# Strassen for half of a right-half stage in a 2048 x 2048 matmul with RMS norm, with B's sums and the loads of A moved to make room

## The chip, the cores and the metric

One core of one Trainium2 chip. The metric is the device time of the kernel in microseconds (us). The kernel before takes 224.39 us, the median of 3 runs (224.3 to 224.49). The engines are named as in the profile: PE is TensorE (matmuls), DVE is VectorE, ACT is ScalarE, POOL is GpSimd and SP is SyncE, which here only issues DMAs: the DMA transposes, nearly all stores of the result, and one load at the start.

## The reference

```python
# a: 2048 x 2048, b: 2048 x 2048, gamma: 2048, all float32; eps = 1e-5
def reference(a, b, gamma, eps):
    x = np.matmul(a, b)
    rms = np.sqrt(np.mean(x ** 2, axis=-1, keepdims=True) + eps)
    return (gamma * x / rms).astype(np.float32)
```

## The kernel before

A has 16 row blocks of 128 rows. The result has four chunks of 512 columns; chunks 0 and 1 are the left half, 2 and 3 the right half. A matmul takes a 128x128 block of A (transposed) and 128x512 of B.

The kernel has three parts. In the **left stage** row blocks 0 to 3 are multiplied with the left half of B as it arrives from memory. In the **right stage** the same row blocks are multiplied with the right half of B, again as it arrives. After that all of B is resident, and the row blocks 4/5, 6/7, ... 14/15 are computed in **pairs** by Strassen's scheme: a pair of row blocks and one half of the columns form a 2x2 matrix of 1024-deep pieces, and seven products of 8 matmuls replace eight. "Pair 4/5, second half" below means row blocks 4 and 5 with the right half of B.

The products are the usual ones: product 1 is (A11+A22)(B11+B22), 2 is (A21+A22)B11, 3 is A11(B12-B22), 4 is A22(B21-B11), 5 is (A11+A12)B22, 6 is (A21-A11)(B11+B12), 7 is (A12-A22)(B21+B22). So each pair needs sums of A (`a_sums`, VectorE), and each half of B needs sums of B once. Sums for products 1, 3 and 4 are kept apart (`b_sums`); those for 6 and 7 overwrite B12 and B21 in place (`b_sums_in_place`) when nothing needs the original any more.

The right stage of before, which the change replaces:

```python
    later = ([("b", kp) for kp in range(5)]
             + [("a", HB), ("b", 5), ("b", 6), ("a", HB + 1), ("b", 7)])   # order of loads
    ...
    groups2 = [(r, c) for r in range(HB) for c in (2, 3)][:-1]
    for kp in range(KP):                     # KP = 8 pieces of B's right half
        load_later(1)
        ...
        stream(groups2, kp, before)          # 14 plain matmuls per piece
        square(squares[kp][0], x_chunk(*squares[kp]))
        ...                                  # sums of B
    ...
    bank = new_bank()                        # the last group, 16 matmuls, after the others
    for kt in range(KT):
        ...
        head_matmul(bank, r3, 3, kt)
    ...
    finish(0, (1, 0))                        # scale and store row block 0
```

One Strassen pair. A bank is a PSUM accumulator of 128x512; `hooks` puts the work for other row blocks between the products, and so fixes its place in the order of each engine:

```python
    def group_half(g, j, hooks):
        x11, x12, x21, x22 = (...)           # the four 128x512 chunks of the result
        t = x22
        at_hook(0)
        p2, p5 = new_bank(), new_bank()
        product(g, j, 2, p2)
        c = spare if (g, j) == (G0, 0) else t
        nc.scalar.copy(out=c, in_=p2)                                      # ScalarE
        ...
        product(g, j, 5, p5)
        nc.vector.tensor_tensor(out=t, in0=p5, in1=c, op=ALU.add)          # VectorE
        ...
        p1 = new_bank()
        product(g, j, 1, p1)
        nc.vector.tensor_tensor(out=t, in0=p1, in1=t, op=ALU.subtract)
        at_hook(3)
        product(g, j, 4, p2, start=False)    # accumulates onto p2, after the copy above
        nc.scalar.copy(out=x21, in_=p2)
        ...
        product(g, j, 3, p5, start=False)    # accumulates onto p5, after the add above
        ...
```

The two reuses of a bank: product 4 may start only when ScalarE has copied product 2, and product 3 only when VectorE has added product 5.

The preparation of a later row block, and its place in pair 4/5:

```python
    def row_norm(mb):     # ScalarE: sum of squares of the block's rows, square root
    def row_factor(mb):   # VectorE: a power of two for each row
    def row_apply(mb):    # ScalarE: scale the rows to fp16
    def apply(mb):
        row_apply(mb)
        transpose_dma(mb)                    # nc.sync.dma_start_transpose
    ...
                hook(0, row_factor, nxt)     # nxt = 6, in the first half of pair 4/5
                hook(1, row_norm, nxt + 1)
                hook(1, apply, nxt)
                hook(2, a_sums, g, (7, 6))
                hook(2, row_factor, nxt + 1)
                hook(2, finish, 1)
                hook(3, squares2, 2)
                hook(4, apply, nxt + 1)      # block 7's DMA transpose
                hook(4, finish, 2)
    ...
    def load_after(g, mb):                   # in the second half: A of blocks 8 and 9
        wait_for(x_chunk(2 * g + 1, 1)[:, 0:1])
        load_block(mb)
```

`finish(mb)` takes the root of the row's mean square (`take_rms`: a reduction on VectorE, a root on ScalarE), scales both halves by it and by gamma (two VectorE instructions of 1.28 us) and stores them through SP.

## Time and profile before

| | before |
|---|---|
| time, median | 224.39 us |
| span of the profiled run | 222.6 us |
| PE busy | 211.1 us, 95% of the span |
| pair 4/5 starts on PE | 69.25 us |
| pair 6/7 starts on PE | 93.63 us |

From the page of the kernel before: busy time by engine, the clock granted to TensorE in 40 slices of the span (9 is full), and the chain of work that ended last, by engine and by line.

```profile
PE 211.1 (95%) x1043; PEld 98.6 (44%) x1043; DVE 161.8 (73%) x324; ACT 129.1 (58%) x272; POOL 24.5 (11%) x49
PEclk9999999999999999999999999999999999999997
PE 83%; DMA 8%; DVE 2%; POOL 2%; issue 1%; ACT 1%; DVEq 0%; ACTq 0%; POOLq 0%
```

The waits of PE in the kernel before: the line that waited, what for, then the total in us, how often, and the longest.

```profile
PE acc L138 <- DVE sq L129: 1.5, 1, 1.5
PE tbank L148 <- POOL msq L198: 1.2, 1, 1.2
PE acc L350 <- DMA b<-in_b_dram: 0.4, 1, 0.4
PE tbank L382 <- DVE head_at L170: 0.4, 1, 0.4
```

These are all at the start, the last ends at 24.7 us, and they sum to 3.5 us. After that the view lists no wait of PE, and its clock is full in every slice but the last. So the kernel is bound by PE: a matmul saved should show in the time, and so should any new wait.

The timeline of PE in the kernel before, around pair 4/5 (start and length in us, then the matmuls and their number):

```profile
69.25 3.62 PE L279 MATMUL acc<-b,s 128*128 128x512 bf16 x16
84.84 1.89 PE L279 MATMUL acc<-early,s 128*128 128x512 bf16 x8
86.57 3.77 PE L279 MATMUL acc<-early,at_even 128*128 128x512 bf16 x16
90.18 7.07 PE L279 MATMUL acc<-b,s 128*128 128x512 bf16 x32
97.08 1.89 PE L279 MATMUL acc<-t_left,s 128*128 128x512 bf16 x8
```

The first line is products 2 and 5 of pair 4/5, where the right stage has ended. The next three are its second half: product 1 at 84.84, products 4 and 3 at 86.57, and from 90.18 products 7 and 6, which are followed without a gap by products 2 and 5 of pair 6/7. Sixteen matmuls take 3.45 us, so pair 6/7 starts at 93.63. Product 1 of pair 6/7 starts at 97.08.

The two DMA transposes of row blocks 6 and 7 in the kernel before, as SP issued them (the second number is the time SP was held):

```profile
77.38 2.03 SPq L186 DMA_TRANSPOSE head_at<-head_at  x1
82.89 1.71 SPq L186 DMA_TRANSPOSE head_at<-head_at  x1
```

By the trace's records of landings, block 7's landed at 87.18, 4.3 us after its issue and 6.4 us before pair 6/7 starts. The loads of A that follow were issued after that, at 88.37. A later transpose of the same size met such loads (a line of SP's timeline and one of POOL's, the kernel before):

```profile
108.41 3.40 SPq L186 DMA_TRANSPOSE at_even<-head_at  x1
110.44 1.05 POOL L115 DMA_DIRECT2D a<-in_a_dram  x2 [0.37 <-issue]
```

This one landed at 116.38, 8.0 us after its issue. It cost PE nothing there, as its rows were not wanted yet.

### The profile page before, as it was taken

Reading aid. Unit: us, or ns where it says so; the run is one execution under the profiler, and the core shown is the slowest. Engines: PE = TensorE matmul, PEld = TensorE weight load, DVE = VectorE, ACT = ScalarE, POOL = GpSimd, SP = SyncE. Lnnn points to the kernel's source line nnn. Section 1 sums busy time; section 2 is a strip of 40 time slices with the busy share of each in tenths; the row PEclk is TensorE's granted clock in tenths of the full one; section 3 lists DMA queues with packets and bytes.
Section 4 is the critical chain, followed back from the end, with each engine's and each line's share of the span. In section 5 each row is a group of like instructions: output and inputs, shape, how many; then the busy total and the mean of one; then the engine's idle time right before and its main releaser. Section 6 shows DMA issues by size and latency. Waiting matters only on the chain.

```text
span 222.6 us, 3026 instructions
## 1 busy us (share of the span) xinstructions
PE 211.1 (95%) x1043; PEld 98.6 (44%) x1043; DVE 161.8 (73%) x324; ACT 129.1 (58%) x272; POOL 24.5 (11%) x49
## 2 busy tenths in 40 slices
PE   7899999999999999999999999999999999999950
PEld 2445444444454444444444444444444444444430
DVE  2427557983999989978949298837994589587692
ACT  3110002807698895799646985699478954334570
POOL 7534232300000001000100002000200000000000
PEclk9999999999999999999999999999999999999997
DMA  6999999999973499818889259945994794044045
GB/s 184 223 202 209 203 208 211 212 303 259 327 280 159 188 272 292 310 72 226 276 228 400 58 174 222 366 151 143 246 368 168 97 282 189 0 188 193 0 190 188
DMA packets 36176, 47.13 MB, mean 212 GB/s; under 512 B 21952, under 2 KB 26048, under 8 KB 34496
## 3 DMA queue, kind: packets, MB, share of 16 engines
q0 software_dynamic: 9648, 23.33, 41.6%
q1 hardware_dynamic: 26080, 22.29, 33.0%
q10 hardware_dynamic: 432, 1.31, 2.0%
q8 instruction: 8, 0.13, 0.2%
q14 instruction: 8, 0.07, 0.1%
HBM read 34.60 MB, written 16.78 MB: 231 GB/s over the span
## 4 chain that ended last, share of the span: by engine, by line
PE 83%; DMA 8%; DVE 2%; POOL 2%; issue 1%; ACT 1%; DVEq 0%; ACTq 0%; POOLq 0%
PE acc L279 63%; PE acc L350 18%; DMA b<-in_b_dram 8%; POOL early L106 1%; DVE x L617 1%; POOL b L100 1%; DVE x L620 1%; PE tbank L179 1%; PE tbank L382 1%; PE tbank L165 1%; ACT sq L291 0%; DVEq L732 0%; ACT sq L682 0%; DVE x L690 0%; DVE r L322 0%
## 5 line engine op out<-in xcount | busy, mean ns | idle before, releaser
L279 PE MATMUL acc<-b,s 128*128 128x512 bf16 x376 | 83.3, 379 | 0.0
L279 PEld LDWEIGHTS <-s 128*128 128x128 f16 x472 | 46.2, 98 | 55.7 <-DVE s L244 0.2
L350 PE MATMUL acc<-b,head_at 128*128 128x512 bf16 x240 | 55.1, 379 | 0.6 <-DMA b<-in_b_dram 0.4
L291 ACT ACTIVATE sq<-x 128x512 bf16<-128x512 f32 x62 | 39.1, 631 | 10.9 <-DVE x L520 5.1
L340 DVE SCALAR_TENSOR_TENSOR x<-x,r,gamma_sb 128x1024 f32<-128x1024 f32 x28 | 34.7, 1282 | 0.8
L209 ACT ACTIVATE sq<-a 128x1024 bf16<-128x1024 f32 x24 | 25.4, 1057 | 16.8 <-DMA a<-in_a_dram 16.4
L350 PEld LDWEIGHTS <-head_at 128*128 128x128 bf16 x240 | 22.9, 98 | 26.7 <-issue 1.1
L393 ACT COPY x<-acc 128x512 f32<-128x512 f32 x11 | 5.9, 591 | 25.1 <-PE acc L350 25.1
L231 ACT ACTIVATE head_at<-a,s 128x2048 f16<-128x2048 f32 x10 | 19.9, 1990 | 0.0
L279 PEld LDWEIGHTS <-at_even 128*128 128x128 f16 x96 | 9.4, 98 | 11.5 <-issue 0.4
L279 PEld LDWEIGHTS <-head_at 128*128 128x128 f16 x96 | 9.4, 98 | 11.3
L100 POOL DMA_DIRECT2D b<-in_b_dram x15 | 10.6, 708 | 16.0 <-DMA b<-in_b_dram 13.2
L217 DVE TENSOR_SCALAR s<-norm 128x1 f32<-128x1 f32 x12 | 1.8, 150 | 14.3 <-ACT norm L212 14.2
L244 DVE TENSOR_TENSOR s<-at_even 128x1024 f16<-128x1024 f16 x15 | 9.7, 684 | 2.8 <-DMA at_even<-head_at 2.8
L291 ACT ACTIVATION_READ_ACCUMULATOR sq<-x 128x1 f32 x62 | 11.7, 188 | 0.0
L279 PE MATMUL acc<-t_left,s 128*128 128x512 bf16 x48 | 11.3, 379 | 0.0
L279 PE MATMUL acc<-early,s 128*128 128x512 bf16 x48 | 11.3, 379 | 0.0
L279 PE MATMUL acc<-early,at_even 128*128 128x512 bf16 x48 | 11.0, 379 | 0.0
L279 PE MATMUL acc<-t_left,at_even 128*128 128x512 bf16 x48 | 10.9, 379 | 0.0
L509 ACT COPY x<-acc 128x512 f32<-128x512 f32 x10 | 5.7, 575 | 8.9 <-PE acc L279 8.9
L279 PE MATMUL acc<-t_left,head_at 128*128 128x512 bf16 x48 | 10.8, 379 | 0.0
L279 PE MATMUL acc<-early,head_at 128*128 128x512 bf16 x48 | 10.8, 379 | 0.0
(86 smaller groups left out, 205.8 us busy)
## 6 DMA issues: line engine op xcount, KB each, us to landing
out_dram<-x SPq DMA_DIRECT2D x30, 512.0 KB, 3.1
a<-in_a_dram POOLq DMA_DIRECT2D x12, 1024.0 KB, 8.5
b<-in_b_dram POOLq DMA_DIRECT2D x15, 512.0 KB, 17.1
early<-in_a_dram POOLq DMA_DIRECT2D x7, 256.0 KB, 14.8
early<-in_b_dram ACTq DMA_DIRECT2D x2, 512.0 KB, 5.9
gamma_sb<-in_gamma_dram POOLq DMA_DIRECT2D x1, 1024.0 KB, 19.9
out_dram<-x SPq DMA_DIRECT2D x3, 256.0 KB, 3.5
early<-in_a_dram SPq DMA_DIRECT2D x1, 512.0 KB, 5.7
```

Of the source, the lines that this page charges most:

```text
L100: nc.gpsimd.dma_start(out=raw[j][kp], in_=b[kp * W2:(kp + 1) * W2, j * HALF:(j + 1) * HALF].rearrange("(t p) n -> p t n", p=P))
L106: nc.gpsimd.dma_start(out=ah(kp), in_=a[0:HB * P, kp * W2:(kp + 1) * W2].rearrange("(r p) k -> p r k", p=P))
L165: nc.tensor.matmul(view[:, t, r, :], ah(kp)[:, r, t * P:(t + 1) * P], identity, is_transpose=True, start=(t == 0 and r == 0), stop=(t == 1 ...
L209: nc.scalar.activation(out=junk, in_=a32[mb][:, h * HALF:(h + 1) * HALF], func=ACTF.Square, scale=2.0 ** -8, accum_out=n2[:, h:h + 1])
L231: nc.scalar.activation(out=a16[mb], in_=a32.pop(mb), func=ACTF.Copy, scale=factor.pop(mb))
L244: nc.vector.tensor_tensor(out=s_sum[s], in0=x, in1=y, op=op)
L279: nc.tensor.matmul(bank, lhsT[:, kp, :], rhs, start=(start and kp == 0), stop=(kp == KP - 1), skip_group_check=not start)
L291: nc.scalar.activation(out=sq[:, 0:CH], in_=src, func=ACTF.Square, scale=inv_sqrt_n, accum_out=msq[mb][:, c:c + 1])
L340: nc.vector.scalar_tensor_tensor(out=x, in0=x, scalar=r, in1=gamma_sb[:, h * HALF:(h + 1) * HALF], op0=ALU.mult, op1=ALU.mult)
L350: nc.tensor.matmul(bank, head_at[:, kt, r, :], head_rhs(c, kt), start=(kt == 0), stop=(kt == KT - 1))
L393: copy(out=x_chunk(*g), in_=banks[g])
L509: nc.scalar.copy(out=x21, in_=p2)
```

## The change

The right stage computed 8 groups (4 row blocks, 2 chunks) with 16 matmuls each, 128 in all. The change computes row blocks 0 and 1 as before (64 matmuls) and row blocks 2 and 3 as a Strassen pair (7 x 8 = 56): 120 matmuls, 8 fewer. Of its seven products, 2, 5 and 1 need no finished in-place sums, so they stream with B as it lands; 4, 3, 7 and 6 come after the last piece. To have time for the sums on VectorE, the in-place sums of B's left half move into the left stage. B's right half is loaded before row blocks 4 and 5, not interleaved with them; so the preparation of 4 and 5, the squares, and everything queued behind them, moves later. The core of the diff:

```diff
-    later = ([("b", kp) for kp in range(5)]
-             + [("a", HB), ("b", 5), ("b", 6), ("a", HB + 1), ("b", 7)])
+    later = [("b", kp) for kp in range(KP)] + [("a", n) for n in range(4)]
 ...
         if kp > 0:
             b_sums(0, kp - 1)
+        if 0 < kp < KP - 2:
+            b_sums_in_place(0, kp - 1)
+        if kp == 4:
+            a_sums(PAIR, (2, 5, 1), 0, 5)
 ...
+    def stream_right(kp):
+        order = [(g, kt) for kt in (2 * kp, 2 * kp + 1) for g in plain]
+        ...
+            for m in (2, 5):
+                pair_matmul(m, kp)
+            if kp > 0:
+                pair_matmul(1, kp - 1)
 ...
+    product(PAIR, 1, 4, pair[2], start=False)
+    row_norm(HB)
+    row_norm(HB + 1)
+    ...
+    product(PAIR, 1, 3, pair[5], start=False)
+    row_apply(HB)
+    ...
+    product(PAIR, 1, 7, p7, within={5: [lambda: turn(HB, 0)]})
+    ...
+    product(PAIR, 1, 6, p6)
 ...
             if g == G0:
-                hook(0, row_factor, nxt)
-                hook(1, row_norm, nxt + 1)
-                hook(1, apply, nxt)
+                hook(0, pair_sums)
+                hook(1, square_half, 1, 1)
+                hook(1, row_norm, nxt)
+                hook(2, pair_ends)
                 hook(2, a_sums, g, (7, 6))
-                hook(2, row_factor, nxt + 1)
-                hook(2, finish, 1)
-                hook(3, squares2, 2)
-                hook(4, apply, nxt + 1)
-                hook(4, finish, 2)
-                hook(6, b_sum_7, 1, KP - 1)
+                hook(2, row_factor, nxt)
+                hook(2, row_norm, nxt + 1)
+                hook(2, apply, nxt)
+                hook(2, finish, 0, (1, 0))
+                hook(3, square_half, r2, 1)
+                hook(3, row_factor, nxt + 1)
+                hook(3, finish, 1)
+                hook(4, row_apply, nxt + 1)
+                hook(4, finish, r2)
+                hook(7, transpose_dma, nxt + 1)
```

The last line is a detail. In the first half of pair 4/5 the changed kernel keeps an intermediate (`t`, and the copy `c`) in `spare`, a buffer that lies inside `head_at`, in the space that block 7's transposed rows will fill. So block 7's DMA transpose can't be issued before the last VectorE add of that half has read it.

## The prediction

> **What bounds it now.** TensorE. The page gives PE 95% busy; the chain of waits follows PE without a gap from 24.7 to 209.5 us, 0.2158 us per 128x512 matmul (91 in 19.64 us). [...] PE's waits after 24.7 us are about zero, so every PE stall or saved matmul there counts in full. VectorE and ScalarE run at 85-95% between 60 and 110 us (table by windows).
>
> **What the change does.** The right half goes from 128 matmuls to 64 + 7x8 = 120: minus 8 x 0.216 = -1.7 us. Transposes (32) stay. B's right half now arrives before blocks 4, 5. One 1.28 us activation-table load leaves the middle; left in-place sums (0.68 us each) move into the first stage; b_sum_6 and b_sum_7 vanish.
>
> **Costs on the critical path** (estimates: durations from the trace of before, summed along each engine's order; [...] the trace shows no reordering there):
>
> 1. First stage: three 128x640 A sums (about 0.4 us each) stand on VectorE before the head-transpose copy. Its bank is needed 3.46 us into the 3.9 us iteration; the copy would end at 4.5. PE stall about 1.0 us.
> 2. Right stage: B lands every 2.48 us, PE uses 2.38; VectorE is full but keeps ahead. No stall. Block 4's scaling then ends about 0.7 us after PE wants to transpose it inside product 7: 0.5-0.8 us.
>    So block pair 4/5 starts about where it did (69.3 us): the gain is spent.
> 3. Pair 4/5 (start S). On ScalarE after product 5: copy, half square 1.18, both row norms 2.57 each, scaling 1.95; only then (S+10.8) the root for block 0. On VectorE finish(0) (2.5), a subtraction, row factor (0.7) and the sum for block 1 wait for it; ScalarE's next root waits for those, about 3 us idle (S+12 to S+15). Then finish(1), scaling of block 7, finish(2). The left half's evictions stand behind these, so in the second half product 4 waits for ScalarE's copy of product 2 (done S+20 to 21.7, wanted S+17.3), and product 3 for VectorE's add (done S+24.2, wanted S+19.0). Loss about 5.2 us.
> 4. Block 7's DMA transpose now starts only after the last add of the first half (S+24), together with the next A loads; it took 4.2-8.0 us in before. Next pair's A sums wait: 0-3 us, estimate 1.0.
>
> Sum: -1.7 + 1.0 + 0.7 + 5.2 + 1.0 = +6.2, giving about 230.4 us. Later groups repeat as before, shifted.
>
> **Predicted: 230.4 us, 80% range 226.5 to 233.5. Faster by over 2%: 0.02; within 2%: 0.22; slower by over 2%: 0.76.**
>
> **What would show it.** PE waits: about 1 us for the transposed head copy (first stage); under 1 us for block 4's scaled rows; several us on the copy of product 2 and the add of product 5 in pair 4/5's second half; perhaps 0-3 us before the next pair. ScalarE: a wait of about 3 us for the sum of squares of block 1. PE gap-free elsewhere, 8 matmuls fewer. PE busy share falls to about 92%.
>
> **What would make it wrong.** If blocks 6, 7 or the roots arrive earlier than my order says, or bank and buffer releases are looser, item 3 shrinks and the time is 224-226; without any stall it is 222.7. If block 7's transpose collides fully with loads, or blocks 6, 7 land after S+6, it is 232-234.

## The result, and the profile after

The changed kernel is correct and took 235.28 us, the median of 4 runs (234.22 to 235.55), beside 224.41 us for the kernel before on the same chip. The ratio is 1.0476, with a 95% interval of 1.0454 to 1.0499: slower by 4.8%. (A ratio here is the mean time of one kernel's fast runs over the mean of the other's of the same rounds, so it is not quite the ratio of the medians quoted.) The direction was predicted; the size was not: 235.28 lies above the range of 226.5 to 233.5.

From the page of the changed kernel:

```profile
PE 213.6 (91%) x1035; PEld 98.4 (42%) x1035; DVE 168.1 (72%) x331; ACT 128.0 (55%) x263; POOL 25.6 (11%) x55
PEclk9999999999999997988999999999999999999996
PE 50%; DMA 4%; DVE 3%; ACT 1%; issue 0%; DVEq 0%; ACTq 0%
```

PE has 8 instructions fewer, as intended, yet it was busy for 2.5 us longer. Here that points to the clock: the granted clock is below 9 in three slices of the middle. And the chain that ended last now runs through a DMA in the middle: the page's next line, by lines, puts its 4% down to `head_at<-head_at`, a transpose. (The 8% of before were the loads of B at the start.)

The waits of PE in the changed kernel that before had not (of the third line, 0.4 us stood in before too):

```profile
PE acc L288 <- ACT x L562: 3.9, 1, 3.9
PE acc L288 <- DVE s L263: 3.8, 1, 3.8
PE tbank L403 <- DVE head_at L176: 1.2, 2, 0.8
PE tbank L188 <- DVE head_at L243: 0.2, 1, 0.2
```

The timeline of PE in the changed kernel, at the marks shown of before (in square brackets: the idle time before the line, and what ended it):

```profile
68.89 3.73 PE L288 MATMUL acc<-b,s 128*128 128x512 bf16 x16
84.54 1.89 PE L288 MATMUL acc<-early,s 128*128 128x512 bf16 x8
90.36 5.31 PE L288 MATMUL acc<-early,at_even 128*128 128x512 bf16 x16 [3.93 <-ACT x L562]
95.50 3.62 PE L288 MATMUL acc<-b,s 128*128 128x512 bf16 x16
102.95 5.31 PE L288 MATMUL acc<-b,s 128*128 128x512 bf16 x16 [3.83 <-DVE s L263]
108.10 1.89 PE L288 MATMUL acc<-t_left,s 128*128 128x512 bf16 x8
```

Set beside the marks of before, these give the account of the loss:

| mark on PE | before | after | behind by | added in this step |
|---|---|---|---|---|
| pair 4/5 starts | 69.25 | 68.89 | -0.36 | -0.36 |
| pair 4/5, second half, product 7 starts | 90.18 | 95.50 | 5.32 | +5.68 |
| pair 6/7 starts | 93.63 | 102.95 | 9.32 | +4.00 |
| pair 6/7, product 1 starts | 97.08 | 108.10 | 11.02 | +1.70 |
| end of the span | 222.6 | 233.7 | 11.1 | +0.1 |

**The first stages (-0.36).** The 8 matmuls saved are worth 1.7 us, and most is spent at once: in the left stage PE waits 0.85 us at 33.0 us for the copy of a transposed block (`head_at L176`), behind the new sums of A on VectorE, and 0.24 us for block 4's scaled rows (`L243`).

**Pair 4/5 (+5.68).** In the second half product 4 could not start until ScalarE had copied product 2. The lines of ScalarE's waits (68 to 112 us) that lead there, in the changed kernel:

```profile
ACT rms L340 <- DVE tot L338: 3.1, 1, 3.1
ACT x L573 <- DMA out_dram<-x: 1.3, 1, 1.3
```

ScalarE waited from 80.7 to 83.8 us to take the root for block 1, since VectorE was scaling block 0 first, and then 1.3 us for a store to free a chunk. The copies of the left half, the scaling of block 7 and the copy that PE needs stand behind these in ScalarE's order, so the latter ran at 89.74. VectorE's add of product 5 (done 93.72) came later still, and product 3 started right after it, at 93.78.

**The start of pair 6/7 (+4.00).** VectorE waited 7.7 us for block 7's DMA transpose, and PE 3.83 us behind VectorE. VectorE's wait (68 to 112 us), SP's two issues of transposes, and the time from issue to landing of the one between 90 and 106 us (the last number), in the changed kernel:

```profile
DVE s L263 <- DMA head_at<-head_at: 7.7, 1, 7.7
79.61 2.09 SPq L198 DMA_TRANSPOSE head_at<-head_at  x1
93.19 2.05 SPq L198 DMA_TRANSPOSE head_at<-head_at  x1
head_at<-head_at SPq DMA_TRANSPOSE x1, 9.0
```

The transpose was issued at 93.19, after the last add, and landed at 102.17, 9.0 us later. The loads of A for blocks 8 and 9 were issued at 93.72, beside it, and landed at 101.53 and 104.0.

**The clock (+1.70).** PE did the first 16 matmuls of pair 6/7 in 5.31 us in place of 3.6. The table of windows of the changed kernel (window; its length, PE busy, PEld, DVE, ACT and POOL busy; then PEclk, the clock granted, the DMA engines' busy share, and GB/s):

```profile
100.00:102.00 2.00, 0.00 (x0) 0.00 (x0) 0.00 (x0) 0.39 (x1) 0.00 (x0) 1.00 1.04 426
102.00:104.00 2.00, 1.05 (x5) 0.48 (x6) 1.80 (x3) 1.94 (x5) 0.00 (x0) 0.92 0.27 111
104.00:106.00 2.00, 2.00 (x6) 0.69 (x5) 1.90 (x4) 0.39 (x2) 0.00 (x0) 0.50 0.03 8
106.00:108.00 2.00, 2.00 (x8) 0.84 (x7) 1.97 (x6) 1.70 (x5) 0.00 (x0) 0.72 0.01 4
108.00:110.00 2.00, 2.00 (x11) 0.88 (x9) 1.31 (x7) 1.73 (x3) 0.00 (x0) 1.00 0.00 0
```

PE idles through the first window while the DMA engines are full (426 GB/s), and 0.8 us after it starts again its clock is halved; in narrower windows the half clock lasts from 103.7 to 107.1. Half speed for 3.4 us costs 1.7 us, the size of the step. Product 4 of pair 4/5 also ran at half clock after its wait of 3.93 us (5.31 us for 16 matmuls from 90.36; there the half clock had begun about 0.3 us before PE resumed), but that was hidden: it ended when VectorE's add did, at about 93.7, and product 3 had to wait for that add in any case.

### The profile page after: what moved, and what is told of

Its sections match the earlier page's. It is cut to its first block, busy times and chain, and to the rows that moved or that the text cites. A ratio compares the mean times of both kernels' runs of the same rounds, so it can differ in the third digit from the quotient of the medians.

```text
span 233.7 us, 3014 instructions
## 1 busy us (share of the span) xinstructions
PE 213.6 (91%) x1035; PEld 98.4 (42%) x1035; DVE 168.1 (72%) x331; ACT 128.0 (55%) x263; POOL 25.6 (11%) x55
## 4 chain that ended last, share of the span: by engine, by line
PE 50%; DMA 4%; DVE 3%; ACT 1%; issue 0%; DVEq 0%; ACTq 0%
PE acc L288 50%; DMA head_at<-head_at 4%; DVE x L684 1%; DVE x L687 1%; ACT sq L306 1%; DVE s L263 0%; DVEq L799 0%; DVE x L584 0%; DVE head_at L580 0%; ACT sq L749 0%; DVE x L757 0%; DVE r L344 0%; ACT rms L350 0%; DVE part L752 0%; DVE both L680 0%
## 5 line engine op out<-in xcount | busy, mean ns | idle before, releaser
L288 PE MATMUL acc<-b,s 128*128 128x512 bf16 x408 | 93.9, 384 | 3.8 <-DVE s L263 3.8
L288 PEld LDWEIGHTS <-s 128*128 128x128 f16 (+1 forms) x512 | 50.2, 99 | 65.2 <-DVE s L263 4.7
L372 PE MATMUL acc<-b,head_at 128*128 128x512 bf16 x176 | 41.9, 379 | 0.5 <-DMA b<-in_b_dram 0.4
L306 ACT ACTIVATE sq<-x 128x512 bf16<-128x512 f32 x54 | 34.0, 630 | 8.1 <-DVE x L684 3.0
L372 PEld LDWEIGHTS <-head_at 128*128 128x128 bf16 x176 | 16.8, 98 | 20.1 <-issue 1.2
L263 DVE TENSOR_TENSOR s<-head_at 128x1024 f16<-128x1024 f16 (+3 forms) x23 | 13.3, 614 | 7.7 <-DMA head_at<-head_at 7.7
L288 PEld LDWEIGHTS <-head_at 128*128 128x128 f16 (+1 forms) x112 | 11.0, 98 | 13.2
L288 PE MATMUL acc<-early,head_at 128*128 128x512 bf16 x64 | 14.5, 379 | 0.0
L288 PE MATMUL acc<-early,s 128*128 128x512 bf16 x56 | 14.4, 379 | 0.0
L279 DVE TENSOR_TENSOR b<-b 128x1024 bf16<-128x1024 bf16 x16 | 10.8, 687 | 0.2
L288 PE MATMUL acc<-t_left,at_even 128*128 128x512 bf16 x48 | 10.8, 379 | 0.0
```

Of the source, the lines that this page charges most:

```text
L263: nc.vector.tensor_tensor(out=sum_of(g, s)[:, lo:hi, :], in0=x[:, lo:hi, :], in1=y[:, lo:hi, :], op=op)
L279: nc.vector.tensor_tensor(out=flat[:, 1:3, :], in0=flat[:, 1:3, :], in1=flat[:, 0::3, :], op=ALU.add)
L288: nc.tensor.matmul(bank, lhsT[:, kp, :], rhs, start=(start and kp == 0), stop=(kp == KP - 1), skip_group_check=not start)
L306: nc.scalar.activation(out=sq[:, 0:CH], in_=src, func=ACTF.Square, scale=inv_sqrt_n, accum_out=msq[mb][:, c:c + 1])
L372: nc.tensor.matmul(bank, head_at[:, kt, r, :], head_rhs(c, kt), start=(kt == 0), stop=(kt == KT - 1))
```

## The experiments

The theory after reading the trace was: of the 11.1 us, some 5.7 come from block 7's transpose (late issue, collision with the loads of A, and the half clock that the wait brings on), and some 5.7 from the order of work in pair 4/5. The rivals were that the transpose is slow by itself; that PE was to arrive late anyway, so that the wait only hides another; and that the half clock is set by something other than the wait. All kernels below are correct. Times are medians of fast runs beside runs of the kernel before on the same chip, which lay between 224.35 and 224.57 us. The changed kernel itself was not run again beside them. Its four runs spread from 234.22 to 235.55 us, so the time alone does not tell a gain of less than about 1 us from none.

### The transpose issued early (e1)

The difference `d` gets a PSUM bank in place of `spare`, and the last sum goes to `x22`; so nothing reads the buffer late, and the transpose follows the scaling of block 7.

```diff
-        nc.vector.tensor_tensor(out=t, in0=p1, in1=t, op=ALU.subtract)
+        d = ps_t.tile([P, CH], FP32, name="tbank") if first else t
+        nc.vector.tensor_tensor(out=d, in0=p1, in1=t, op=ALU.subtract)
+        t = x22
 ...
-                hook(4, row_apply, nxt + 1)
+                hook(4, apply, nxt + 1)
                 hook(4, finish, r2)
-                hook(7, transpose_dma, nxt + 1)
```

> Edit: the difference of product 1 goes to a free PSUM bank, so block 7's DMA transpose need not wait for the last add of the first half of pair 4/5 and is issued right after block 7's scaling. Theory (late start of the transpose costs the wait of VectorE's A sums before pair 6/7, 4.0 us on TensorE, and the half clock after that wait, 1.7 us): the transpose is issued near 88.5 us and lands before 95; no wait on the A sums at the start of pair 6/7; the 3.9 us wait of product 4 stays; 229.2 to 230.2 us. Rival (the wait is the fault of the A loads of blocks 8, 9 or of a full VectorE, not of the late start): a wait of over 2 us stays there, 233 us or more.

Measured: 229.96 us (229.72 to 231.05), ratio 1.0259. SP issued the transpose at 88.59, it landed at 92.88, before the loads of A were issued (93.76), the wait for the sums of A at pair 6/7 is gone, and PE is free of gaps from 95.54 at full clock. Product 4's wait stays.

```profile
88.59 1.71 SPq L198 DMA_TRANSPOSE head_at<-head_at  x1
PE acc L288 <- ACT x L562: 3.9, 1, 3.9
```

The first line is SP's timeline of e1, the second one of PE's waits of e1. One edit returned 5.3 us of the 10.9, close to the 4.00 + 1.70 of the account. So the late transpose and the clock after it are one cause, and nothing waited behind it.

### The loads of A after the transpose (e2)

The loads of blocks 8 and 9 wait until block 7's transpose has landed; the transpose still starts late.

```diff
-        wait_for(x_chunk(2 * g + 1, 1)[:, 0:1])
+        wait_for(at(2 * g + 3)[:, 0, 0:1] if g == G0 else x_chunk(2 * g + 1, 1)[:, 0:1])
         load_block(mb)
```

> Edit: the loads of blocks 8, 9 wait until block 7's transpose has landed; the transpose starts as late as in the changed kernel. Theory (the transpose took 9.0 us instead of about 4.5 because these loads ran at the same time): issue to landing 4.3 to 5.2 us, no wait on the A sums, but block 8's row norm comes 2 us later and the copy of product 2 of pair 6/7 behind it makes product 4 there wait 2 to 3 us: 231.5 to 233 us. Rival (the transpose is slow by itself at this place, or because of the output stores before it): 8 to 9 us again, 235 us or more.

Measured: 234.48 us (234.24 to 234.74), ratio 1.0451 (1.0435 to 1.0467), so only 0.8 us gained, which is within the spread. The mechanism came out as the theory had it: alone, the transpose was issued at 93.06 and landed at 97.31, 4.25 us in place of 9.0. It is not slow by itself. In the changed kernel the loads' packets ran beside it: from its issue to its landing (93.2 to 102.2 us) the queue of the loads took 53.5% of the time of the 16 DMA engines and SP's queue, the transpose and the end of a store, 38.3%. But the time expected (231.5 to 233) was missed. The transpose's time from issue to landing and the timeline of PE in e2:

```profile
head_at<-head_at SPq DMA_TRANSPOSE x1, 4.2
90.23 6.28 PE L288 MATMUL acc<-early,at_even 128*128 128x512 bf16 x16 [3.94 <-ACT x L562]
107.27 1.89 PE L288 MATMUL acc<-t_left,head_at 128*128 128x512 bf16 x8 [2.12 <-ACT x L562]
```

The loads came later by as much: block 8 landed at 104.0, and ScalarE, which had to read it before the copy that PE needs, made product 4 of pair 6/7 wait 2.12 us. And the half clock after product 4's first wait lasted longer in this run: 6.8 us, until 95.6, in place of 3.4 us, until 93.5, by the trace's clock records. So 16 matmuls took 6.28 us and no longer fit under the wait for VectorE. The collision was gone, but the wait had moved to another transfer.

### Keeping PE busy through the wait (e3, and again e11)

Sixteen useless matmuls before pair 6/7 fill the wait, to ask whether it is the wait that halves the clock.

```diff
+        if (g, j) == (G0 + 1, 0):
+            idle = ps_t.tile([P, CH], FP32, name="tbank")
+            for _ in range(16):
+                nc.tensor.matmul(idle, identity, raw[0][0][:, 0, :CH], start=True, stop=True)
         p2, p5 = new_bank(), new_bank()
```

> Edit: 16 matmuls of no use (into a bank nobody reads) stand before pair 6/7, inside the 3.8 us wait for the A sums. Theory (TensorE's clock was halved after the wait and this costs 1.7 us on the 8 products that follow): granted clock 1.0 in the first products of pair 6/7, the A sums come at the same moment, 233.4 to 233.9 us. Rival (the slow matmuls have another cause, for instance the loads or a lasting throttle): clock 0.5 there again and 235.1 to 235.5 us.

Measured: 234.76 us (234.55 to 235.18), ratio 1.046; 0.5 us gained, within the spread, and 0.9 above the upper end of what was expected. The timeline of PE in e3:

```profile
98.97 3.62 PE L562 MATMUL tbank<-b,identity 128*128 128x512 bf16 x16
103.88 3.63 PE L288 MATMUL acc<-b,s 128*128 128x512 bf16 x16 [1.29 <-DVE s L263]
```

With the filler, which left 1.29 us of the wait, the same 16 matmuls took 3.63 us in place of 5.31, at a granted clock of 1.00 (103.9 to 107.5 us): here it was the idle time that cost the clock, and the term of 1.7 us is real. But they started 0.9 us later than in the changed kernel, since the transpose landed at 103.10 and not at 102.17. Did the filler do that? The same kernel was run again for one look:

> The same kernel as e3 again. In e3 the clock was full as expected but the A sums came 0.9 us later than in the changed kernel, so little was gained. Chance: the transpose lands within 0.4 us of 102.2 this time and the time is 233.4 to 233.9 us. Cause in the filler (matmuls that read SBUF slow the transpose): it lands at 103 us or later again.

Measured: 234.09 us (one run, state unknown). Here the transpose landed at 101.79, and pair 6/7 started at 103.30 right behind the filler, again at full clock (3.62 us). So the 0.9 us of e3 came from run to run, and the filler need not delay the transpose. But this time product 4's half clock of the half before lasted longer (6.35 us for 16 matmuls), PE came to the filler 0.9 us later than in e3, and then the filler itself held pair 6/7 up: VectorE began its sums at 101.82, so that they would have let pair 6/7 start at about 102.6. What remains is that the same 16 matmuls take between 5.3 and 6.35 us after such a wait. In the clock records of the profiles the phase is 3.4 us long (the changed kernel, e1, e3, e10, e12) or 6.8 us (e2, e8, e11).

### The roots earlier (e4, and e10)

This takes up the other half of the loss. The roots for blocks 0 and 1 are taken before the row norms of blocks 6 and 7, so that ScalarE need not wait 3.1 us for VectorE.

```diff
-        a_sums(G0, (2, 1))
+        a_sums(G0, (2,))
+        take_rms(0)
+        a_sums(G0, (1,))
 ...
                 hook(1, row_norm, nxt)
+                hook(1, take_rms, 1)
```

> Edit: the sums of squares and roots of blocks 0 and 1 are taken before the row norms of blocks 6 and 7 instead of after block 6's scaling. Theory (the ping-pong of roots and finishes between ScalarE and VectorE delays the copy of product 2 and the add of product 5 in the second half of pair 4/5): ScalarE's 3.1 us wait for the sum of block 1 goes, product 4's wait falls from 3.9 to about 0.6 us, the loss in that half from 5.7 to 1.0 to 2.0 us; the wait before pair 6/7 stays about 3.8 us since the transpose moves along: 230.6 to 231.8 us. Rival (the row norms and scaling of the late blocks 6, 7 alone fill ScalarE): product 4's wait stays above 3 us, 234.5 us or more.

Measured: 236.26, 233.75 and 234.11 us in the fast runs, ratio 1.0461 with 1.0405 to 1.0517: a plain miss of the 230.6 to 231.8 expected. (A fourth run, the profiled one, took 379.86 us at a mean clock of 0.56; it is a slow run and is left out.) A fast profile was needed to see why, so the same kernel ran again for one look:

> The same kernel as e4, whose profiled run was slow, for a profile in the fast state. Theory (block 0's stores queue behind block 6's transpose on SyncE): SyncE issues block 0's stores after 79.5 us although VectorE finished them before; ScalarE's copy of product 4 in the first half waits for a store and starts at 84 us or later; product 4's wait in the second half 2.5 to 4 us; 233.5 to 236 us. Rival (the row norms fill ScalarE): the copy starts late with ScalarE busy until then.

Measured: 235.44 us (one run, state unknown). Two lines of ScalarE's waits in e10, and SP's issues:

```profile
ACT x L575 <- DMA out_dram<-x: 4.7, 1, 4.7
ACT rms L340 <- DVE tot L338: 1.7, 1, 1.7
79.67 2.10 SPq L198 DMA_TRANSPOSE head_at<-head_at  x1
81.83 9.95 SPq L365 DMA_DIRECT2D out_dram<-x  x6
```

The wait for the root shrank from 3.1 to 1.7 us, and a wait of 4.7 us took its place: ScalarE's copy into a chunk whose old content, block 0's result, had not been stored. VectorE scaled it from 76.48 to 78.96, but in SP's order block 6's transpose stood ahead of the stores, and that one waits for the scaled rows of block 6. The stores were issued at 81.83.

### The roots earlier, and block 0's stores ahead of the transpose (e5)

The kernel of e4 with one swap:

```diff
-                hook(2, apply, nxt)
                 hook(2, finish, 0, (1, 0))
+                hook(2, apply, nxt)
```

> Edit: as e4, and block 0's finish (with its output stores) stands before block 6's scaling and transpose in program order. Reason: in e4 the stores of block 0 still queue on SyncE behind block 6's transpose, which waits for block 6's scaling (79.6 us), and ScalarE's copy of product 4 waits for such a store to land before it may write that slot; so e4 moved the roots but not the stores. Theory (roots and stores together make the ping-pong): ScalarE's copy of product 4 in the first half at 80.5 to 81.5 us instead of 85.3; product 4's wait in the second half under 1 us, product 3's about 1 us; the wait before pair 6/7 stays near 3.8 us with the half clock after it: 230.3 to 231.8 us. Rival (row norms and scaling of the late blocks fill ScalarE by themselves): product 4's wait stays above 3 us, 234 us or more.

Measured: 230.40 us (229.66 to 232.27), ratio 1.0281. SP issued block 0's stores at 78.39, and product 4 waited 1.6 us in place of 3.9 (under 1 had been expected). One of ScalarE's waits and a line of PE's timeline in e5:

```profile
ACT x L564 <- DMA out_dram<-x: 2.1, 1, 2.1
98.81 3.63 PE L288 MATMUL acc<-b,s 128*128 128x512 bf16 x16 [3.25 <-DVE s L263]
```

So the second part of the loss is the order in two queues: ScalarE behind VectorE's scaling, and the stores behind a transpose. Removing the first alone (e4) returned about nothing, both returned 4.9 us. The stores alone, without the earlier roots, were not tried, so their share is open. The wait for the sums of A stayed, at 3.25 us, as it should; but against the expectation it left the clock full in the profiled run (3.63 us for 16 matmuls). So the 4.9 us hold part of the term of the clock too: the two runs with a mean granted clock of 0.99 took 229.66 and 230.12 us, the two with 0.98 took 230.67 and 232.27. By the marks used above, in the profiled run (230.12) the step of pair 4/5 fell from 5.68 to 1.65 us, the wait for the transpose from 4.00 to 3.42, and the clock from 1.70 to 0.01.

### The stall of the left stage (e8)

The early sums of A are placed behind the copies of the transposed head blocks, in iterations 5 and 6.

```diff
+        if kp in (5, 6):
+            before.append(lambda: a_sums(PAIR, ((2,), (5, 1))[kp - 5], 0, 5))
 ...
-        if kp == 4:
-            a_sums(PAIR, (2, 5, 1), 0, 5)
```

> Edit: of the changed kernel only the early A sums of blocks 2, 3 are moved behind the head-transpose copies of iterations 5 and 6. Theory (they stall TensorE in the first stage by 0.85 us plus 0.3 us for the issue): pair 4/5 starts about 1 us earlier and everything behind it too: 234.0 to 234.6 us. Rival (the stall is covered, since the first stage is paced by the arrival of B): same time as the changed kernel, 235.0 us or more.

Measured: 233.91 us (233.42 to 234.39), ratio 1.0425, 1.4 us better than the changed kernel and 0.1 below the range expected. The stall of 0.85 us is gone and pair 4/5 starts at 67.98 in place of 68.89. The rest came from the clock, in the profiled run. The transpose was as slow as in the changed kernel (9.0 us, and VectorE waited 7.7 us for it), but the half clock after product 4's wait lasted 6.8 us, so PE came to pair 6/7 later, waited only 1.63 us there, and its clock stayed full. A line of PE's timeline in e8:

```profile
102.05 3.63 PE L288 MATMUL acc<-b,s 128*128 128x512 bf16 x16 [1.63 <-DVE s L263]
```

### Both causes removed (e6)

e5 and e1 together.

> Edit: e5 and e1 together. Theory: the two losses are all of the regression in pair 4/5 and its start of pair 6/7, and they add: 225.0 to 226.2 us, no PE wait over 1.2 us after 69 us, granted clock 1.0 throughout. Rival (something else keeps TensorE waiting, for instance later loads of A): 227.5 us or more.

Measured: 226.75 us (226.18 to 227.07), ratio 1.0103. Slightly above the 225.0 to 226.2 expected. One of ScalarE's waits in e6, and SP's issue of block 7's transpose:

```profile
ACT x L564 <- DMA out_dram<-x: 2.4, 1, 2.4
84.01 4.14 SPq L198 DMA_TRANSPOSE head_at<-head_at  x1
```

Block 7's transpose is now issued early, right behind block 1's stores, and its issue held SP for 4.14 us. ScalarE's copy of product 2 waited 2.4 us for the second of these stores (landed at 87.47), and PE 1.9 us, where no wait over 1.2 us had been expected. The early transpose is not the main reason: e5, without it, waited 2.1 and 1.6 us at the same place. Still, 8.5 of the 10.9 us have come back: the two causes are most of the loss.

### Towards a version that is faster than before (e7, e9, e12)

e7 adds to e6 the edit of e8, moves block 2's and part of block 1's finishing to other places, and turns block 4's rows later within product 7, so that the 0.24 us wait goes too.

```diff
-    product(PAIR, 1, 7, p7, within={5: [lambda: turn(HB, 0)]})
+    product(PAIR, 1, 7, p7, within={7: [lambda: turn(HB, 0)]})
 ...
-                hook(3, finish, 1)
+                hook(3, finish, 1, (1, 0))
                 hook(4, apply, nxt + 1)
-                hook(4, finish, r2)
+                hook(4, take_rms, r2)
 ...
                 hook(1, square_half, r3, 1)
+                hook(2, finish, r2)
```

> Edit: e6, and: block 2's finish moved into the second half, block 1's right half stored first, block 4's first transposes two matmuls later, the early A sums of blocks 2, 3 behind the head-transpose copies of the next two iterations. Theory: with the stalls gone the 8 saved matmuls (1.7 us) show: 222.6 to 224.0 us, 0.2 to 0.8% faster than before. Rival (arrival of B holds the right stage back once the first stage no longer stalls): TensorE waits on B there and the time is 224.2 us or more.

Measured: 227.31 us (226.87 to 227.85), ratio 1.0124, a miss of over 3 us. The rival, that PE would wait for B, shows only as one wait of 0.43 us, at 56.8. Up to the start of pair 6/7 the plan worked: pair 4/5 starts at 68.07, pair 6/7 at 93.03, which is 0.6 us ahead of the kernel before. Then it was lost. The transpose was issued at 83.33 and the loads of A, now released earlier as well, at 86.17; the transpose landed at 92.26, 8.9 us after its issue, a store of block 2 at 99.92, and product 4 of pair 6/7 waited 2.28 us for a chunk that this store held.

e9 takes e7, lets the loads wait for the transpose as in e2, and finishes block 2's right half first:

```diff
-        wait_for(x_chunk(2 * g + 1, 1)[:, 0:1])
+        wait_for(at(2 * g + 3)[:, 0, 0:1] if g == G0 else x_chunk(2 * g + 1, 1)[:, 0:1])
 ...
-                hook(2, finish, r2)
+                hook(2, finish, r2, (1, 0))
```

> Edit: e7, and: the loads of blocks 8, 9 wait for block 7's transpose to land (as e2), and block 2's right half is stored first. Reason: in e7 block 7's transpose again ran together with these loads (8.9 us) and the store of block 2's right half landed only at 99.9 us, which made product 4 of pair 6/7 wait 2.3 us. Theory: transpose 4.3 to 5.5 us, store landed before 95, no PE wait over 0.8 us after 69 us: 223.0 to 224.2 us. Rival (the output stores and A loads of this stretch are too many for the DMA engines in any order): 225.5 us or more.

Measured: 226.63 us (226.16 to 227.96, 6 runs), ratio 1.0118 with 1.0095 to 1.0141: above the 223.0 to 224.2 expected, and where the rival had put it (225.5 or more). A line of PE's timeline in e9:

```profile
99.04 1.89 PE L288 MATMUL acc<-t_left,head_at 128*128 128x512 bf16 x8 [1.57 <-ACT x L564]
```

Pair 6/7 starts at 92.13, 1.5 us ahead of before; but block 8's load, which waits its turn, landed at 95.78. ScalarE waited 5.6 us for it, and the copy that PE needs stood behind it: 1.57 us. A pair later the sums of A came 0.59 us late.

e12 takes e9 and lets block 8's load go as soon as its buffer is free; only block 9's waits.

```diff
-                hook(0, load_after, g, nxt + 2)
-                hook(0, load_block, nxt + 3)
+                if g == G0:
+                    hook(0, load_block, nxt + 2)
+                    hook(0, load_after, g, nxt + 3)
+                else:
+                    hook(0, load_after, g, nxt + 2)
+                    hook(0, load_block, nxt + 3)
```

> The kernel of e9 with one change: block 8's load no longer waits for block 7's transpose but goes as soon as its buffer is free (estimate about 78 us, when block 6's scaling has read it); only block 9's load waits for the transpose. If what held e9 back was the late landing of block 8 (95.78 us, 5.6 us of waiting on ScalarE, 1.57 us on TensorE before product 4 of pair 6/7), block 8 lands before 90 us, that wait of 1.57 us goes, and the time is 224.5 to 225.6 us. Rival: the load only moves the collision; it stretches block 7's transpose (5.9 us in e9) or the stores of block 1, the wait returns elsewhere, and the time is 226 us or more.

Measured: 227.80 us (227.61 to 228.01), ratio 1.0142: the rival was right. One line of ScalarE's waits in e12, SP's issue of block 7's transpose, and PE's timeline:

```profile
ACT x L564 <- DMA out_dram<-x: 4.0, 1, 4.0
83.56 5.58 SPq L198 DMA_TRANSPOSE head_at<-head_at  x1
88.62 5.14 PE L288 MATMUL acc<-early,at_even 128*128 128x512 bf16 x16 [3.47 <-ACT x L564]
```

Block 8 landed at 85.58, its wait and the one of 1.57 us are gone. But the load, issued at 78.72, now lies beside block 6's transpose and the stores of block 1: block 6's transpose took 8.3 us in place of 4.9, block 1's first store, which landed at 84.51 in e9, landed at 87.91, the copy of product 2 in pair 4/5 waited for it, PE waited 3.47 us, and the half clock came back (5.14 us for 16 matmuls).

No version tried is faster than the kernel before. Four orders of the same transfers (e6, e7, e9, e12) each cost PE a wait of 1.6 to 3.5 us, in one of two places: before product 4 in the second half of pair 4/5 (e6, e12: a store of block 1) or before product 4 of pair 6/7 (e7: a store of block 2; e9: the load of block 8). Whether some order of transposes, loads and stores fits and brings in the 1.7 us of saved matmuls was not settled.

## Why the prediction was right or wrong

It had the direction, the two places and most of the mechanism, and it was wrong in one term of its sum and by one term that it lacked.

- **The matmuls saved, and items 1 and 2: right.** Predicted to cancel and leave pair 4/5 where it was, at 69.3 us; measured 68.89. The stall of "about 1.0 us" in the left stage was 0.85, and block 4's turn cost 0.24 where 0.5 to 0.8 was predicted. e8 moved the sums of A and the stall went.
- **Item 3: right in place and size, but it lacked one queue.** "Loss about 5.2 us" measured 5.68. ScalarE's wait of "about 3 us" was 3.07. With S = 68.89, the copy of product 2 was done at S+21.4 (predicted S+20 to 21.7) and the add of product 5 at S+24.8 (predicted S+24.2). The argument took ScalarE and VectorE to work in the order of the program, as in the trace of before (the 27 instructions of ScalarE from 70.34 to 84.26 us all stand in that order), and the agreement fits that. What the prediction had not seen is that SP's order binds as well: e4 and e10 show that the roots alone change about nothing, as the stores of block 0 stand behind block 6's transpose; with both moved (e5) the step of 5.68 fell to 1.65 us.
- **Item 4: wrong; this is the step that failed.** "Block 7's DMA transpose now starts only after the last add of the first half (S+24), together with the next A loads; it took 4.2-8.0 us in before. Next pair's A sums wait: 0-3 us, estimate 1.0." The start was right (issued at 93.19, S+24.3). The size was not: the wait was 4.00 us. The trace of before held the answer: the 8.0 us were those of the transpose that met two loads of A (issued at 108.41, shown above), the 4.3 us those of one that met none, and the prediction itself says that this one would run with the loads. It did not say which of the two cases this was, and its 1.0 lies near the low end of its own 0 to 3. Beside the loads it took 9.0 us, alone (e2) 4.25 us. At 4.25 us it would have landed at 97.4, and PE was ready for pair 6/7 at 99.1. The trace of before held the other number too: in its view of the DMA from 76 to 98 us the two loads of A take 24.9% of the engines' 22 us, which is 5.5 us. So the estimate should have been the time of all three transfers together, about 9.8 us (an estimate: those 5.5 and the 4.3 us of the transpose that met no load), and not that of one; measured, the last of the three landed 10.8 us after the transpose's issue.
- **A term that was missing: +1.70.** The wait of 3.83 us on PE was followed by half clock for 3.4 us. The prediction had no term for this behind the waits that it had itself predicted, and the trace of before has no wait of PE over 1.5 us that could have shown one; its clock is halved only at the end, where PE has no work left (0.50 from 220 to 222.6 us). e3 and e11 filled the wait and the clock stayed full. With 4.00 and 1.70 in place of 1.0 the sum is 10.9 with the prediction's other terms, against 10.9 measured between the medians (0.36 too much in the first terms and 0.48 too little in item 3 nearly cancel).
- **"If block 7's transpose collides fully with loads ... it is 232-234": nearly.** It did collide, and without the clock the time would have been 233.6 by the account (235.28 - 1.70). Treating that as a tail put the range below the result.

e1 shows that item 4 and the clock are worth 5.3 us together, e5 that item 3 with the clock is worth 4.9, e6 that all are worth 8.5. The last is less than the sum of the first two, 10.2. At least part of the difference is the clock's 1.7 us, which both of them hold (e5 in its two faster runs): either edit alone can make the wait before pair 6/7 too short for the half clock. The rest was not traced.

## What to carry to other kernels

When a change delays a transfer that used to run alone, ask what it will run beside, and cost all of them together on the DMA engines (here 4.25 us alone, 9.0 us beside two loads of 1 MB with the engines busy for 0.92 of the time); a range of durations in the trace of before is not chance to take a middle from, but two cases to tell apart. In the profiled runs here a wait of TensorE of 3.25 us (e5) left the clock full, and one of 3.47 us (e12) did not; a wait forecast near these lengths must be priced with and without the half-speed phase behind it, 1.5 to 2.7 us more for the 16 matmuls here. If the wait's length is unsure, that is a step in the time, not a slope. So two remedies that each shorten the wait both seem to earn that step, and their gains must not be added. On a kernel whose main engine is 95% busy, 8 saved matmuls (1.7 us) were worth less than one reordered queue: list the order of each queue before and after, SP's queue of stores and transposes included.

## What the runs show of transposes and the clock, and what stays open

- The cost of a transpose's neighbours: a 128x2048 fp16 transpose took 4.25 us alone (e2), and beside two loads of 1 MB 8.0 us in the kernel before, 9.0 in the changed kernel and 8.9 in e7.
- The issue of a transpose held SP for 2.05 us in the changed kernel, where the DMA engines fell idle meanwhile (a busy share of 0.01 from 93.6 to 94.0 us), for 4.14 us in e6, right behind block 1's stores, and for 5.58 us in e12, where the DMA engines were busy for 8 tenths or more of each slice of the view from 78 to 90 us; in e6 the next stores in SP's order were issued as it ended, at 88.25 us.
- No half clock came after the gaps of at most 2.3 us (e7, e9), nor after one of 3.25 us (e5), but it came after gaps of 3.47 us (e12) and 3.7 to 4.1 us (the changed kernel, e1, e2, e3, e8, e10, e11). The two phases after waits in the changed kernel cost PE 1.7 us each, together 1.4% of its span, and the one on the path was as large as the whole gain that the change aimed at. The phase was not one length: 3.4 or 6.8 us by the clock records, and the same 16 matmuls took 5.14 to 6.35 us. It was 6.8 us where PE idled for 0.9 to 1.4 us within its first 3.4 us (e2, e8, e11) and 3.4 us where it idled for about 0.3 us or less (the changed kernel, e1, e3, e10); no run was made to test that.
- What caused the one run of 379.86 us (e4), with one core in use, in which the granted clock was 0.56 from about 5 us to the end, stays open.
